# Modulation sums moved from TensorE to VectorE, ScalarE and GpSimd, with longer pauses in background work

## Chip, cores and metric

The kernel runs on one core of one Trainium2 chip. The metric is the device time of one execution in microseconds (us); the figure quoted for a kernel is the median of its runs.

## What is computed

A trunk of two layers works on 256 latent tokens and 256 context tokens of width 1024. Each layer is a gated feed-forward network (FFN), a token-mixing block with four branches (latent attention, windowed attention, a state-space branch called S5, a gated MLP), and a second FFN. Each of these three sub-layers is modulated: a vector made from the conditioning input gives a shift, a scale and a gate of 1024 numbers, one set for latent tokens and one for context tokens. The change concerns how these vectors are made.

```python
mod_l = (silu_c  @ w_ada[l] + b_ada[l]).reshape(b, N_MOD, D_MODEL)      # 9 vectors of 1024 per layer
mod_c = (silu_cc @ w_ada[l][:, :n_mod_c * D_MODEL] + ...)               # 9 in layer 0, 5 in layer 1
def modulated_norm(xs, gain, mod, s):
    return rms_norm(xs, gain) * (1.0 + mod_vec(mod, 3 * s + 1)) + mod_vec(mod, 3 * s)
def gated_residual(xs, y, gain, mod, s, weight):
    return xs + weight * mod_vec(mod, 3 * s + 2) * rms_norm(y, gain)
def ffn_sublayer(xs, mod, s, g_pre, g_post, w_in_f, w_out_f):
    a, g = jnp.split(modulated_norm(xs, g_pre, mod, s) @ w_in_f, 2, axis=-1)
    return gated_residual(xs, (jax.nn.silu(a) * g) @ w_out_f, g_post, mod, s, MACARON_WEIGHT)
```

`w_ada[l]` is 1024 x 9216 in fp32, so each vector reads 4 MB of weights for two rows of activations.

## The kernel before, in words

**Matrix products.** Every large product splits its fp32 operands into a high and a low part and adds three TensorE matmuls (`mm3`, L285 to L287). Weights come in raw tiles of 1 MB over the SP queue (`Ring.pump`, L166). `Ring.ahead` lets ScalarE copy the high part (L208) and VectorE, or GpSimd in the mixing block, subtract it for the low part (L211), up to two pieces ahead of the product that uses them; there are two raw slots and three slots of parts.

**The FFN** (`ffn`, L623) walks 44 blocks of 128 hidden columns. A block is 24 matmuls of 512 columns, and after each half of them `tick` adds 2.6 to `K.clock`. Every second block is followed by `evacuate`: ScalarE SiLU (L655), VectorE product (L659), ScalarE copy (L661), VectorE subtraction (L662). Then `natural_out` multiplies by `w_out`.

**Background work** is written as generators. `tick` (L256) steps each task whose wake time on `K.clock` has come; a task's `yield 2.5` asks for 2.5 of that clock. The clock only orders the program: each engine then runs its own instructions in that order and waits on semaphores. `finish` (L266) steps a task to its end at once.

**Modulation** (`Ada`, L307). A sum over 1024 rows is cut into four chunks of 256 rows. A chunk is one 1 MB load on SP (L320) and four matmuls of 512 columns (L341); the stationary operand holds the two activation columns, and the four matmuls lie side by side in the array. ScalarE evacuates the sum (L347). A shift or scale is then turned by four transposes and two VectorE additions (L364 to L366); a gate goes through four selection matmuls (L382), two VectorE operations (L384, L385) and GpSimd DMAs to DRAM (L388), from where `load_gate` (L392) spreads it. The vectors of sub-layer 0, shift and scale, are made before the first FFN; the other 56 chunks run inside three FFNs: 24 in layer 0's first, 28 in layer 0's second, 12 in layer 1's first; 8 of the 24 are shift and scale of sub-layer 1.

**S5 tables** (`s5_prep`, L1065) are built in the background of each layer's first FFN: VectorE and GpSimd complex products (`cmul`, L98), transposes of the GpSimd results `p_xr` and `p_xi` (L292), and GpSimd DMAs to a DRAM table `tab` (L1129, L1143, L1155). Layer 0's preparation also has the discretisation, of which eight steps are taken ahead of the first FFN. In the mixing block `s5_run` (L1173) reads the table back in four groups `r_tq` (L1189), the first two over SP, and feeds TensorE (L1225). `mla`, `gqa` and `s5_glu` are further background tasks of `mix` (L696).

**Where the time lies.** First FFN about 45 to 460 us, mixing 460 to 890, second FFN 890 to 1330, layer 1's first FFN 1330 to 1745, its mixing 1745 to 2040, its last FFN 2040 to the end.

Of the kernel before, what the change touches and what calls it, by code (L numbers as in the profile page):

```python
# [298 lines left out]
def aux_tile(K):  # L299
    return K.ps_aux.tile([P, 512], F32, tag="aux", name="aux")  # L300
# [6 lines left out]
class Ada:  # L307


    def __init__(self, K, places, jobs):  # L310

        self.K, self.places, self.jobs = K, places, jobs
        self.chunks = [(l, c, k) for l, s, kind, _ in jobs
                       for c in ((3 * s, 3 * s + 1) if kind == "norm" else (3 * s + 2,)) for k in range(0, 8, 2)]
        self.loaded = self.n = 0
# [8 lines left out]
    def run(self, every, bank=aux_tile):  # L324
        self.every, self.bank = every, bank
        self.pump()
        yield every[0]
        for l, s, kind, weight in self.jobs:
            yield from (self.norm(l, s) if kind == "norm" else self.gate(l, s, weight))
# [39 lines left out]
    def gate(self, l, s, weight):  # L369

        K, nc, v, q = self.K, self.K.nc, self.K.nc.vector, self.K.nc.gpsimd
        c0 = (3 * s + 2) * D
        ev = yield from self.sums()
        bp = t2k(K, "bp")
        v.memset(bp, 0.0)
        for st in range(2):
            nc.sync.dma_start(bp[st:st + 97:32, 0:256], K.b_ada[l, c0:c0 + D].rearrange("(q c) -> q c", q=4))
            nc.sync.dma_start(bp[st:st + 97:32, 256:512], K.norm_post[l, s].rearrange("(q c) -> q c", q=4))
        yield 8.0
        pt = self.bank(K)  # L380
        for k in range(4):
            nc.tensor.matmul(pt[32 * k:32 * k + 32, 0:256], K.sel[:, k // 2, :], ev[:, 256 * (k % 2):256 * (k % 2) + 256], start=True, stop=True,  # L382
                             tile_position=(0, 32 * k))
        v.tensor_tensor(out=ev[:, :256], in0=pt[:, :256], in1=bp[:, 0:256], op=OP.add)  # L384
        v.scalar_tensor_tensor(out=ev[:, :256], in0=ev[:, :256], scalar=weight, in1=bp[:, 256:512], op0=OP.mult, op1=OP.mult)  # L385
        gd = K.dr.tile([2, 4, 256], F32, tag=f"gd{l}{s}", name=f"gd{l}{s}")
        for st in range(2):
            q.dma_start(gd[st], ev[st:st + 97:32, :256])  # L388
        K.gd[l, s] = gd
# [233 lines left out]
def ffn(K, l, s, f, pn, tiles, nxt, jobs, every=(5.0, 7.6), pools=None, prep=False):  # L623
# [8 lines left out]
    with pools.es as es:  # L632
        hb = None
        big = [gp.tile([P, 2, 1024], F32, tag=t, name="ada" + t) for t in ("G", "y1")]
        ada = add_task(K, Ada(K, big, jobs).run(every), 5.0)
# [53 lines left out]
        load_gate(K, l, s, G)  # L689
# [6 lines left out]
def mix(K, l, pn, last, nxt):  # L696
# [67 lines left out]

    def u_out(t, p):
# [20 lines left out]
    def s5_all():  # L786
        out = yield from s5_run(K, l, sp5, A, K.tab[l], K.r8d[l], not last)
        yield from s5_glu(K, l, sp5, *out, Tq, new_branch)

    s5t = add_task(K, s5_all(), 2.0)  # L790
# [274 lines left out]
def s5_prep(K, l, pool, tab, loads=None):  # L1065
# [55 lines left out]
    for qg in range(4):  # L1121
# [8 lines left out]
        if qg < 2:  # L1130
# [11 lines left out]
            yield 2.5  # L1142
# [30 lines left out]
def s5_run(K, l, pool, A, tab, r8d, need_ctx):  # L1173
# [18 lines left out]
    load_tq(0)  # L1192
    yield 4.0
# [18 lines left out]
    load_tq(1)  # L1212
# [98 lines left out]
def s5_glu(K, l, pool, ygT, wh, wl, bg, Tq, new_branch):  # L1311
# [8 lines left out]
    yield 2.5  # L1320
# [139 lines left out]
def mla(K, l, pool, wkv, wq, gk, rm, wqs, nB, nC, ntq, new_branch):  # L1460
# [42 lines left out]
    yield 5.0  # L1503
# [71 lines left out]
def gqa(K, l, pool, nB, nC, ntq, new_branch):  # L1575
# [11 lines left out]
    for src, n in ((nC[:, 0:2, 256:512], 256), (nB[:, 0:2, 160:288], P)):  # L1587
# [9 lines left out]
        yield 3.0  # L1597
# [37 lines left out]
def trace(K, nc, tc, rec):  # L1635
# [4 lines left out]
    with ExitStack() as es:  # L1640
# [18 lines left out]
        K.sel = C([P, 2, 32], "sel")  # L1659
# [15 lines left out]
        nc.vector.memset(K.sel, 0.0)  # L1675
        id4 = K.ident.rearrange("p (a b r) -> p a b r", a=2, b=2)
        nc.vector.tensor_tensor(out=K.sel[:, :, 0:2], in0=id4[:, 0, :, 0:2], in1=id4[:, 1, :, 0:2], op=OP.add)
# [6 lines left out]
        for l in range(2):  # L1684
# [6 lines left out]
                  [(0, 0, "norm", None)])  # L1691
        for i, _ in enumerate(ada.run((0.0, 0.0), mm_tile)):
# [10 lines left out]
            for _ in range((1, 1, 1, 1, 2, 2, 0, 0, 0)[min(i, 8)]):  # L1703
                pools.ptask.step(0.0)
# [12 lines left out]
        for l in range(2):  # L1717
            last = l == 1
            jobs = [(0, 0, "gate", 0.5), (0, 1, "norm", None), (0, 1, "gate", 1.0)] if l == 0 else []
            jobs.append((l, 2, "norm", None))  # L1720
            if last:
                jobs.append((l, 2, "gate", 0.5))
            pn = ffn(K, l, 0, 0, pn, range(4), lambda: PreNorm(K, l, 1), jobs, (7.6, 7.6) if last else (5.0, 7.6), pools, True)
            pools = None
            pn = mix(K, l, pn, last, lambda: PreNorm(K, l, 2))
            if last:
                ffn(K, l, 2, 1, pn, range(2), None, [])
            else:
                pn = ffn(K, l, 2, 1, pn, range(4), lambda: PreNorm(K, l + 1, 0), [(l, 2, "gate", 0.5)] + [(l + 1, i, *j) for i, w in ((0, 0.5), (1, 1.0)) for j in (("norm", None), ("gate", w))])
# [65 lines left out]
```

## Time and profile before

| | us |
|---|---|
| median of 3 runs (2238.04 to 2239.87) | 2238.07 |
| the profiled execution's own time | 2238.61 |
| its span, first to last instruction | 2236.8 |
| TensorE busy in it | 2124.8 |
| VectorE busy | 1110.7 |
| ScalarE busy | 764.4 |
| GpSimd busy | 399.5 |

The profile shows one execution. Engines are PE (TensorE matmul), PEld (its weight load), DVE (VectorE), ACT (ScalarE), POOL (GpSimd) and SP (which issues DMAs). "L341" is a line of the kernel. [...]

### The profile page before, as it was taken

The numbers are of one execution on the slowest core, as the hardware profiler recorded it, in microseconds if no ns is written. First come the engines' busy times: TensorE is split into PE (matmuls) and PEld (weight loads), VectorE is DVE, ScalarE is ACT, GpSimd is POOL, SyncE is SP. The second block draws the span as 40 slices with busy tenths as digits, with TensorE's granted clock in tenths as the row PEclk, the third lists the DMA queues.
The fourth block names the chain that finished last, engine by engine and source line by source line (L and its number), as shares of the span: only waits on it lengthen the run. The fifth ranks groups of instructions, "written<-read, shape, count | busy, mean of one in ns | idle before, by whom it ended". The sixth has DMA issues, their size and how long they took to land.

```text
span 2236.8 us, 28936 instructions
## 1 busy us (share of the span) xinstructions
PE 2124.8 (95%) x11691; PEld 1716.4 (77%) x11691; DVE 1110.7 (50%) x1965; ACT 764.4 (34%) x1275; POOL 399.5 (18%) x372
## 2 busy tenths in 40 slices
PE   5899999989999999899999989999999889897998
PEld 3677778877767778777777877778888778787997
DVE  6873332357435655533332357733324585656554
ACT  3222222342533333422222332222222345354443
POOL 1660000022222300100000027500000244442000
PEclk9999999999999999999999998999999999998999
DMA  8566542324322223355554335633323454443554
GB/s 295 179 217 208 184 159 85 128 93 175 98 70 71 83 83 114 114 185 189 173 198 151 114 102 171 228 134 113 104 87 105 168 168 123 125 141 120 182 188 151
DMA packets 211039, 323.12 MB, mean 144 GB/s; under 512 B 15737, under 2 KB 152569, under 8 KB 210905
## 3 DMA queue, kind: packets, MB, share of 16 engines
q1 hardware_dynamic: 196864, 287.17, 38.4%
q0 software_dynamic: 9584, 31.56, 4.3%
q10 hardware_dynamic: 4456, 2.53, 0.5%
q8 instruction: 92, 1.51, 0.3%
q14 instruction: 43, 0.34, 0.0%
HBM read 307.57 MB, written 14.71 MB: 144 GB/s over the span
## 4 chain that ended last, share of the span: by engine, by line
PE 48%; DVE 5%; issue 2%; ACT 1%; DMA 1%; POOL 1%; ACTq 0%; SPq 0%; DVEq 0%; POOLq 0%
PE mm L285 15%; PE mm L286 14%; PE mm L287 14%; PE aux L341 2%; PE aux L292 1%; DMA r_tq<-tab 1%; DVE wlo L211 1%; ACT jk L400 0%; DVE hThi L462 0%; PE aux L1438 0%; ACT h L459 0%; DVE hTlo L463 0%; DVE g_tm L1594 0%; PE aux L1563 0%; DVE xs L433 0%
## 5 line engine op out<-in xcount | busy, mean ns | idle before, releaser
L285 PE MATMUL mm<-hThi,whi 128*128 128x512 f32 (+1 forms) x1992 | 719.6, 361 | 8.7 <-DVE hThi L462 8.4
L286 PE MATMUL mm<-hTlo,whi 128*128 128x512 f32 (+1 forms) x1992 | 703.7, 353 | 7.7 <-POOL hTlo L463 7.3
L287 PE MATMUL mm<-hThi,wlo 128*128 128x512 f32 (+1 forms) x1992 | 701.1, 352 | 0.0
L211 DVE TENSOR_TENSOR wlo<-wraw,whi 128x1024 fp32r<-128x1024 f32 (+1 forms) x285 | 363.2, 1279 | 427.3 <-ACT whi L208 425.6
L285 PEld LDWEIGHTS mm<-hThi,whi 128*128 128x128 f32 x1992 | 382.5, 192 | 119.6 <-issue 49.4
L208 ACT ACTIVATE whi<-wraw 128x1024 fp32r<-128x1024 f32 (+1 forms) x348 | 363.9, 1049 | 237.5 <-PE mm L287 174.5
L286 PEld LDWEIGHTS mm<-hTlo,whi 128*128 128x128 f32 x1992 | 382.3, 192 | 58.7 <-POOL hTlo L463 10.3
L287 PEld LDWEIGHTS mm<-hThi,wlo 128*128 128x128 f32 x1992 | 382.0, 192 | 50.4
L211 POOL TENSOR_TENSOR wlo<-wraw,whi 128x1024 fp32r<-128x1024 f32 (+1 forms) x66 | 162.3, 2467 | 861.4 <-ACT whi L208 821.1
L659 DVE TENSOR_TENSOR sa<-sa,mm 128x512 f32<-128x512 f32 (+1 forms) x88 | 54.3, 617 | 160.2 <-PE mm L287 160.2
L655 ACT ACTIVATE sa<-mm 128x512 f32<-128x512 f32 (+1 forms) x88 | 47.8, 544 | 229.6 <-PE mm L287 229.6
L285 PE MATMUL mm<-whi,ha 128*128 128x512 f32 x308 | 120.0, 389 | 0.0
L286 PE MATMUL mm<-wlo,ha 128*128 128x512 f32 x308 | 119.8, 389 | 0.0
L287 PE MATMUL mm<-whi,ha 128*128 128x512 f32 x308 | 119.8, 389 | 0.0
L661 ACT ACTIVATE ha<-sa 128x512 fp32r<-128x512 f32 (+1 forms) x44 | 25.4, 578 | 228.3 <-DVE sa L659 228.3
L661 ACT ACTIVATE hb<-sa 128x512 fp32r<-128x512 f32 (+1 forms) x44 | 25.4, 578 | 178.3 <-DVE sa L659 169.7
L287 PE MATMUL mm<-whi,hTlo 128*128 128x512 f32 (+2 forms) x224 | 80.9, 361 | 4.4 <-POOL hTlo L463 4.3
L285 PE MATMUL mm<-whi,hThi 128*128 128x512 f32 (+2 forms) x224 | 81.9, 366 | 3.4 <-DVE hThi L462 3.4
L286 PE MATMUL mm<-wlo,hThi 128*128 128x512 f32 (+2 forms) x224 | 80.4, 359 | 1.2 <-DVE wlo L211 1.2
L388 POOL DMA_DIRECT2D gd<-ev x12 | 7.0, 583 | 415.6 <-ACT whi L208 253.4
L285 PE MATMUL mm<-whi,hb 128*128 128x512 f32 x188 | 73.1, 389 | 0.0
L286 PE MATMUL mm<-wlo,hb 128*128 128x512 f32 x188 | 73.1, 389 | 0.0
(446 smaller groups left out, 2909.6 us busy)
## 6 DMA issues: line engine op xcount, KB each, us to landing
wraw<-in_w_ffn_in_dram SPq DMA_DIRECT2D x88, 1024.0 KB
wraw<-in_w_in_dram SPq DMA_DIRECT2D x42, 1024.0 KB
wraw<-in_w_ffn_out_dram SPq DMA_DIRECT2D x40, 1024.0 KB
adaG<-in_w_ada_dram SPq DMA_DIRECT2D x32, 1024.0 KB
aday<-in_w_ada_dram SPq DMA_DIRECT2D x32, 1024.0 KB
ha<-in_w_ada_dram SPq DMA_DIRECT2D x8, 1024.0 KB
wraw<-in_w_out_dram SPq DMA_DIRECT2D x7, 1024.0 KB
r_tq<-tab SPq DMA_DIRECT2D x8, 768.0 KB
```

The lines of the kernel that those rows point to most:

```text
L208: K.nc.scalar.activation(h3, r, AF.Copy)
L211: (self.eng or K.lo_eng).tensor_tensor(out=l3, in0=r, in1=h3.bitcast(F32), op=OP.subtract)
L285: mm(out, ahi, bhi, start=first, stop=False)
L286: mm(out, ahi, blo, start=False, stop=False)
L287: mm(out, alo, bhi, start=False, stop=last)
L292: K.nc.tensor.transpose(out, x, K.ident[:n, :n])
L341: nc.tensor.matmul(ps[o:o + 32, :], self.K.sc[:, k + i, :], w[:, i, 512 * b:512 * b + 512], start=k == 0, stop=k == 6, tile_position=(0, o))
L388: q.dma_start(gd[st], ev[st:st + 97:32, :256])
L655: nc.scalar.activation(sa[:, :N], ps[:, :N], AF.Silu)
L659: nc.vector.tensor_tensor(out=g[:, :N], in0=g[:, :N], in1=ps[:, :N], op=OP.mult)
L661: nc.scalar.activation(hh, g[:, :N], AF.Copy)
```

## The change

Six things change together.

1. `AdaSum` makes 14 of the modulation vectors without TensorE. A step takes 128 rows by 512 columns (256 KB, one SP load into one of four places): VectorE multiplies by the latent activation and adds to an accumulator; for vectors that context tokens need too (`ns` = 2), ScalarE scales the same tile in place and GpSimd adds it to a second accumulator. Sixteen steps make one vector; then `total` sums over partitions with `2 * ns` matmuls against ones. Of the 14, ten have `ns` = 2 and four `ns` = 1. Shift and scale of layer 0's sub-layer 1 stay with `Ada` and go first.
2. Steps are paced by `K.clock`: one per 1.75 in layer 0's first FFN (64 steps), per 1.6 in its second (112 steps, the last 16 with `ns` = 1), per 3.2 in layer 1's first (48 steps, all `ns` = 1).
3. `s5_prep`: the pause ahead of the second group's transposes grows from 2.5 to 11; the `p_xt` table transfers are issued on ScalarE, right after the copy that fills them; five of its steps, not eight, are taken ahead of the first FFN.
4. `s5_run` is started at the head of `mix`, so that the first two table groups are read there.
5. Pauses grow in `s5_glu` (2.5 to 5), `mla` (5 to 10) and `gqa` (3 to 7 for the keys).
6. `load_gate` loads only the streams in use.

```diff
+class AdaSum:
+    def pump(self):
+        while self.loaded < min(self.n + len(self.places), len(self.chunks)):
+            l, c, k, b = self.chunks[self.loaded]
+            c0 = D * c + 512 * b
+            self.K.nc.sync.dma_start(self.places[self.loaded % len(self.places)], self.K.w_ada[l, P * k:P * k + P, c0:c0 + 512])
+            self.loaded += 1
+    def run(self, every):
...
+        due = self.K.clock
+        for l, s, kind, weight, ns in self.jobs:
+            for k in range(8):
+                for b in range(2):
...
+                    if k == 0:
+                        nc.vector.tensor_scalar(out=a[0], in0=w, scalar1=f[0], scalar2=None, op0=OP.mult)
+                    else:
+                        nc.vector.scalar_tensor_tensor(out=a[0], in0=w, scalar=f[0], in1=a[0], op0=OP.mult, op1=OP.add)
+                    if ns > 1:
+                        nc.scalar.activation(w if k else a[1], w, AF.Copy, scale=f[1])
+                        if k:
+                            nc.gpsimd.tensor_tensor(out=a[1], in0=a[1], in1=w, op=OP.add)
+                    self.n += 1
+                    self.pump()
...
+                    due += every
+                    if due > self.K.clock:
+                        yield due - self.K.clock
+            yield 2.5
...
+    def total(self, ns):
+        ps = aux_tile(self.K)
+        for st in range(ns):
+            for b in range(2):
+                o = 64 * st + 32 * b
+                self.K.nc.tensor.matmul(ps[o:o + 32, :], self.K.ones[:, 0:32], self.acc[:, st, 512 * b:512 * b + 512], start=True, stop=True,
+                                        tile_position=(0, o))
+        return ps
...
@@ ffn
-        ada = add_task(K, Ada(K, big, jobs).run(every), 5.0)
+        def modulation():
+            if first:
+                yield from Ada(K, big, first).run((5.0, 7.6))
+            yield from AdaSum(K, [big[0][:, j // 2, 512 * (j % 2):512 * (j % 2) + 512] for j in range(4)], big[1], jobs).run(every)
+        ada = add_task(K, modulation(), 5.0)
...
@@ mix
+    s5g = s5_all()
+    next(s5g)
...
-    s5t = add_task(K, s5_all(), 2.0)
+    s5t = add_task(K, s5g, 6.0)
@@ s5_prep
-            yield 2.5
+            yield 2.5 if qg == 0 else 11.0
...
+        nc.scalar.dma_start(tab[:, gs, 0:256], xt.rearrange("p j k m -> p j (k m)"))
         if qg < 3:
             x = x_table(qg + 1)
         yield 2.5
-        dq.dma_start(tab[:, gs, 0:256], xt.rearrange("p j k m -> p j (k m)"))
@@ s5_run
     load_tq(0)
+    load_tq(1)
     yield 4.0
...
-    load_tq(1)
@@ s5_glu
-    yield 2.5
+    yield 5.0
@@ mla
-    yield 5.0
+    yield 10.0
@@ gqa
-        yield 3.0
+        yield 3.0 if n > P else 7.0
@@ trace, ahead of the first FFN
-            for _ in range((1, 1, 1, 1, 2, 2, 0, 0, 0)[min(i, 8)]):
+            if i in (0, 5, 6, 7, 8):
                 pools.ptask.step(0.0)
```

## Rows read from the trace of the kernel before

**Rows 1.** The page, part 1: busy time, share of the span, instructions.
```profile
PE 2124.8 (95%) x11691; PEld 1716.4 (77%) x11691; DVE 1110.7 (50%) x1965; ACT 764.4 (34%) x1275; POOL 399.5 (18%) x372
```
**Rows 2.** Stretches: length, busy PE, PEld, DVE, ACT, POOL; granted clock; DMA share, GB/s.
```profile
1040.00:1080.00 40.00, 40.00 (x190) 29.53 (x189) 13.83 (x18) 11.45 (x15) 0.00 (x0) 1.00 0.54 185
...
1400.00:1440.00 40.00, 40.00 (x244) 30.27 (x241) 36.55 (x40) 11.70 (x17) 22.46 (x27) 1.00 0.57 187
1440.00:1480.00 40.00, 40.00 (x188) 30.44 (x187) 13.02 (x17) 9.87 (x13) 4.81 (x9) 1.00 0.72 254
...
1600.00:1640.00 40.00, 40.00 (x178) 33.14 (x177) 11.34 (x11) 8.96 (x10) 0.00 (x0) 1.00 0.34 112
```
**Rows 3.** Chain that ended last, around one chunk: start, length, engine and line.
```profile
985.67 1.00 PE aux L341 x8
986.67 0.43 PE mm L285
987.10 0.23 PE mm L286
```
**Rows 4.** Lines L341 and L382: ns min/median/max, first and last start us.
```profile
L341 PE MATMUL aux<-adaG,sc x256: 592/592/617, 58.3 to 1482.8; 128*32 128x512 f32 x128
...
L382 PE MATMUL aux<-ev,sel x48: 379/391/403, 120.6 to 1512.2; 128*32 128x256 f32 x48
```
**Rows 5.** Timeline 1404 to 1412: start, length, engine; in brackets the idle time before.
```profile
1404.16 8.03 DVE L211 TENSOR_TENSOR wlo<-wraw,whi 128x1024 fp32r<-128x1024 f32 x1 [0.26 <-ACT whi L208]
...
1404.52 1.07 POOL L102 TENSOR_TENSOR p_cmg<-p_px,p_B 128x512 f32<-128x512 f32 x1
...
1409.83 1.27 POOL L110 TENSOR_TENSOR p_xi<-p_xi,p_cmgu 128x512 f32<-128x512 f32 x1
```
**Rows 6.** Timeline 1361 to 1366: VectorE while GpSimd works too.
```profile
1362.44 1.76 DVE L102 TENSOR_TENSOR p_cmv<-p_pr,p_C 128x512 f32<-128x512 f32 x1
1364.13 1.77 DVE L103 TENSOR_TENSOR p_cmvu<-p_pr,p_C 128x512 f32<-128x512 f32 x1
```
**Rows 7.** Durations by line, ns min/median/max, of shapes the change adds or meets.
```profile
L211 DVE TENSOR_TENSOR wlo<-wraw,whi x285: 1018/1226/8027, 35.3 to 2222.7; 128x1024 fp32r<-128x1024 f32 x140, 128x832 fp32r<-128x832 f32 x3
...
L662 DVE TENSOR_TENSOR hb<-sa,hb x44: 424/692/693, 223.1 to 2172.3; 128x512 fp32r<-128x512 f32 x33, 128x256 fp32r<-128x256 f32 x11
...
L512 DVE SCALAR_TENSOR_TENSOR x<-z,po_rst,x x20: 751/752/754, 445.9 to 2232.4; 128x512 f32<-128x512 f32 x20
...
L433 DVE TENSOR_SCALAR xs<-x,pn_rst x44: 473/481/2626, 15.4 to 2037.8; 128x512 f32<-128x512 f32 x44
...
L463 POOL TENSOR_TENSOR hTlo<-h,hThi x22: 1258/1276/1394, 37.0 to 2043.9; 128x512 fp32r<-128x512 f32 x22
...
L400 ACT ACTIVATE jk<-x x44: 629/632/637, 10.0 to 2034.7; 128x512 f32<-128x512 f32 x44
```
**Rows 8.** DMA issues: queue, count, KB each, median us from issue to landing.
```profile
wkv<-in_mla_w_ukv_dram POOLq DMA_DIRECT2D x2, 256.0 KB, 3.2
```
**Rows 9.** Table building, TensorE: transposes in both layers and the wait before each.
```profile
112.43 1.11 PE L292 MATMUL aux<-ident,p_xr 128*128 128x128 f32 x4 [9.73 <-POOL p_xr L106]
...
1391.52 1.11 PE L292 MATMUL aux<-ident,p_xr 128*128 128x128 f32 x4 [3.65 <-POOL p_xr L106]
```
**Rows 10.** The same, in stretches: length, busy PE, granted clock, DMA share, GB/s.
```profile
115.00:120.00 5.00, 5.00 (x36) 0.76 0.72 217
...
1390.00:1395.00 5.00, 3.37 (x12) 0.56 0.46 172
```
**Rows 11.** The mixing block: issue of the table reads (ns), and TensorE's waits (us).
```profile
L1189 SPq DMA_DIRECT2D r_tq<-tab x8: 339/427/499, 495.3 to 1766.3; - x8
...
PE px L1225 <- DMA r_tq<-tab: 2.9, 1, 2.9
...
PEld aux L292 <- issue: 6.9, 1, 6.9
...
PEld aux L286 <- DVE g_yl L1319: 1.5, 1, 1.5
```

More of the change, by code (lines that the diff above doesn't have):

```diff
@@ L312, in __init__ @@
         self.K, self.places, self.jobs = K, places, jobs
-        self.chunks = [(l, c, k) for l, s, kind, _ in jobs
-                       for c in ((3 * s, 3 * s + 1) if kind == "norm" else (3 * s + 2,)) for k in range(0, 8, 2)]
+        self.chunks = [(l, c, k) for l, s in jobs for c in (3 * s, 3 * s + 1) for k in range(0, 8, 2)]
         self.loaded = self.n = 0
@@ L327, in run @@
         yield every[0]
-        for l, s, kind, weight in self.jobs:
-            yield from (self.norm(l, s) if kind == "norm" else self.gate(l, s, weight))
+        for l, s in self.jobs:
+            yield from self.norm(l, s)
     def sums(self):
@@ L620, in __init__, with ffn @@
             self.ptask = add_task(K, s5_prep(K, l, pp, K.tab[l], self.loads))
-def ffn(K, l, s, f, pn, tiles, nxt, jobs, every=(5.0, 7.6), pools=None, prep=False):
+def ffn(K, l, s, f, pn, tiles, nxt, jobs, every=1.6, pools=None, prep=False, first=()):
     nc = K.nc
@@ L763, in mix, with s5_all @@
     A = sp5.tile([64, 8, 256], F32, tag="r_A", name="r_A")
+    def s5_all():
+        out = yield from s5_run(K, l, sp5, A, K.tab[l], K.r8d[l], not last)
+        yield from s5_glu(K, l, sp5, *out, Tq, new_branch)
+    s5g = s5_all()
+    next(s5g)
     def u_out(t, p):
@@ L784, in mix @@
         pb.part(t, 0)
-    def s5_all():
-        out = yield from s5_run(K, l, sp5, A, K.tab[l], K.r8d[l], not last)
-        yield from s5_glu(K, l, sp5, *out, Tq, new_branch)
-    s5t = add_task(K, s5_all(), 2.0)
+    s5t = add_task(K, s5g, 6.0)
     pb.run(range(4), 1)
@@ L1658, in trace @@
         K.sc = C([P, 8, 32], "sc")
-        K.sel = C([P, 2, 32], "sel")
+        K.ones = C([P, 64], "ones")
         K.npT = C([P, 2, 3, 8], "npT")
@@ L1674, in trace @@
         nc.scalar.activation(K.sc[:, :, 0:2], pt[:, 0:16].rearrange("p (s b) -> p b s", s=2), AF.Silu)
-        nc.vector.memset(K.sel, 0.0)
-        id4 = K.ident.rearrange("p (a b r) -> p a b r", a=2, b=2)
-        nc.vector.tensor_tensor(out=K.sel[:, :, 0:2], in0=id4[:, 0, :, 0:2], in1=id4[:, 1, :, 0:2], op=OP.add)
+        nc.vector.memset(K.ones, 1.0)
         pt = aux_tile(K)
@@ L1718, in trace @@
             last = l == 1
-            jobs = [(0, 0, "gate", 0.5), (0, 1, "norm", None), (0, 1, "gate", 1.0)] if l == 0 else []
-            jobs.append((l, 2, "norm", None))
+            norm = lambda a, b, ns: [(a, b, "shift", None, ns), (a, b, "scale", None, ns)]
             if last:
-                jobs.append((l, 2, "gate", 0.5))
-            pn = ffn(K, l, 0, 0, pn, range(4), lambda: PreNorm(K, l, 1), jobs, (7.6, 7.6) if last else (5.0, 7.6), pools, True)
+                jobs, first, every = [*norm(1, 2, 1), (1, 2, "gate", 0.5, 1)], (), 3.2
+            else:
+                jobs, first, every = [(0, 0, "gate", 0.5, 2), (0, 1, "gate", 1.0, 2), *norm(0, 2, 2)], ((0, 1),), 1.75
+            pn = ffn(K, l, 0, 0, pn, range(4), lambda: PreNorm(K, l, 1), jobs, every, pools, True, first)
             pools = None
@@ L1728, in trace @@
             else:
-                pn = ffn(K, l, 2, 1, pn, range(4), lambda: PreNorm(K, l + 1, 0), [(l, 2, "gate", 0.5)] + [(l + 1, i, *j) for i, w in ((0, 0.5), (1, 1.0)) for j in (("norm", None), ("gate", w))])
+                jobs = [(l, 2, "gate", 0.5, 2)]
+                for i, w in ((0, 0.5), (1, 1.0)):
+                    jobs += [*norm(l + 1, i, 2), (l + 1, i, "gate", w, 2 - i)]
+                pn = ffn(K, l, 2, 1, pn, range(4), lambda: PreNorm(K, l + 1, 0), jobs)
 def trunk(tc, *args):
```

75 lines of the change are left out of this document (55 added, 20 removed).

## The prediction

> **What bounds the kernel now.** I read the busy times first: TensorE works for 2124.8 us of the 2236.8 us span and no other engine for more than half of it [rows 1]. Cut into stretches of 40 us, the FFNs show TensorE at 40.00 of 40 at full clock with VectorE at 11 to 14, ScalarE at 9 to 11 and GpSimd near 0 [rows 2]. So in an FFN an instruction taken off TensorE is time, as long as the others keep up. What one chunk costs is read from the chain that ended last: the chunk starts at 985.67, the second matmul behind it at 987.10, while two neighbours are 0.23 apart [rows 3]; the chunk holds the stream up by 1.43 - 0.23 = 1.20 us. Then I looked at what VectorE and GpSimd do to each other, because the change makes both work in the FFNs. In the timeline a VectorE subtraction of the usual 1.22 us takes 8.03 and ends at 1412.19, 1.09 us after a run of six GpSimd products that began at 1404.52 and ended at 1411.10 [rows 5, 7]: it stood still for the whole run. Where the two alternate, VectorE's 128x512 products, elsewhere near 0.69 us [rows 7], take 1.76 and end 1.70 apart, a GpSimd product and a VectorE product in turn [rows 6]. Operations with two tensors from SBUF on the one engine and on the other exclude each other here. TensorE never stopped in that stretch (40.00 of 40, VectorE "busy" 36.55) [rows 2], so a VectorE lag of 8.03 - 1.22 = 6.8 us is absorbed by the weight parts made two pieces ahead.
>
> My sum is made against the profiled execution, 2238.6 us (span 2236.8 and 1.8 around it), 0.5 us above the median.
>
> **TensorE's work.** 56 chunks leave: 56 x 1.20 = -67.2. Each of the 14 vectors gets one sum over partitions, at most four fp32 matmuls of 512 columns side by side like a chunk [rows 4], 1.20 each: +16.8. (Four have half of that; I leave them at the full price.) The six gates lose four selection matmuls of 256 columns, 8 of the 48 instructions [rows 4], each set priced at 0.84, between 0.39 (one instruction) and 1.20 (a chunk): -5.0. The transposes stay in number. Together **-55.4**.
>
> **What the new steps cost elsewhere.** With `ns` = 2 a vector has 16 steps; 14 of them are a VectorE multiply-add of two SBUF tensors (nearest row 0.75) and a GpSimd add (1.28); in two VectorE only multiplies (0.48) and GpSimd does nothing [rows 7]. ScalarE's 0.63 per step [rows 7] shares nothing. By the alternating rows a pair takes less than its parts: 1.70 where 0.69 + 1.28 is 1.97, so 0.27 less; I price the pair at 0.75 + 1.28 - 0.27 = 1.76. The mean step is (14 x 1.76 + 2 x 0.48) / 16 = 1.60 us of VectorE and GpSimd together. A block of the FFN is 24 matmuls, and 178 matmuls take 40 us [rows 2]: 5.39 us for 5.2 on the program's clock, 1.037 us each. A block needs besides a weight subtraction (1.22) and half a hidden subtraction (0.35) [rows 7]: 1.57.
> - Layer 0's first FFN: 5.2 / 1.75 = 2.97 steps, 2.97 x 1.60 + 1.57 = 6.32 against 5.39. The 64 steps last 112 of clock, 21.5 blocks: 21.5 x 0.93 = 20.0 too much.
> - Its second: 3.25 steps, 6.77 against 5.39, over 96 steps = 29.5 blocks: 40.7 too much. The last 16 steps have no GpSimd part.
> - Layer 1's first: no GpSimd at all, 1.6 steps x 0.75 + 1.57 = 2.8 of 5.39: hidden.
>
> Of each excess 6.8 us is absorbed, as read above: 13.2 + 33.9 = 47.1. Within a block the engines also wait for each other in order (VectorE for ScalarE's copy, ScalarE's scaling for VectorE, the load for GpSimd), which costs only where both stand idle; I take **+50**, next to the sum of the rows. The bounds: 0, if the lag never uses up the lookahead, and +95, if the ring of four places sets the pace (second rival).
>
> What queues behind these waits: behind the multiply-add on VectorE the weight and hidden subtractions; behind the scaling on ScalarE SiLU and the weight copies; behind the add on GpSimd the gate's DMAs and, early on, table building; on SP each 256 KB load waits for the add that frees its place, and the weight loads stand behind it. The DMA rate is no bound: 256 KB x 3.25 per 5.39 us is 158 GB/s, and weights at 1 MB per two blocks 97; 254 GB/s is what one stretch already moved, at a share of 0.72 [rows 2]. SP issues four times as many loads, 224 for 56, each near 0.43 us [rows 11], about a quarter of its time.
>
> **Table building.** TensorE waits 9.73 us for GpSimd's `p_xr` in layer 0 and 3.65 in layer 1 [rows 9]. Behind each the granted clock is at the lower of its two levels: 0.76 over 115 to 120 [rows 10] is half speed for 2.4 us, and with the 2.6 us from the transposes to 115 some 5.0 us at half, 2.5 lost; in layer 1 half speed for about 3.5 us, 1.7 lost. The pause is 8.5 longer, 8.8 us of other matmuls: layer 0 keeps 0.9 of its wait, -11; layer 1 none, -5. Together **-16**; bounds 0 (the wait returns one group later) and -18. The eight `p_xt` issues leave GpSimd's queue and cost ScalarE about 0.43 us each [rows 11], beside other work.
>
> **Mixing.** The table reads are issued some 20 us earlier, when SP has no weight load due; layer 1's wait of 2.9 goes [rows 11], layer 0's I put at 2 (0 to 2.9). If SP were held by buffers not yet free, weight loads behind it would be late; 0 is the bound. The wait of 6.9 before the key transposes [rows 11] shrinks by 4 x 1.037: -4. `s5_glu`'s 1.5 [rows 11] goes only if the task is not already being finished at once, when pauses count for nothing: -1 (0 to -1.5). `mla`'s longer pause may leave attention work to be stepped without cover in layer 1: +1 (0 to +4). Together **-9**.
>
> **Start.** Three preparation steps move into the first FFN, where VectorE stands ahead of the context normalisation. No row prices them; between -2 and +5, by the 3.45 of 40 us that VectorE had left in its fullest stretch [rows 2], I take **+2**.
>
> Sum: -55.4 + 50 - 16 - 9 + 2 = -28.4, so 2238.6 - 28.4 = **2210 us**, 1.3% faster. About 0.2%, 4.5 us, is what a measurement of this kernel can tell from no change.
>
> **Rivals.**
> - *The excess does not bite.* Then the sum is -78.4: 2160. For it: VectorE lags of 6.8 us that cost TensorE nothing [rows 2, 5]. Against it: the excess comes in every block, not once. 0.18.
> - *Slower: the ring of four places.* The place of step n is loaded again only when its add is done, and VectorE waits at the head of its queue for the load. A round is load 3.2 [rows 8], 0.75, 0.63 and 1.28 [rows 7], and two waits for the other engine (1.28 and 1.22): 8.4 us for four steps, 2.1 each; a load behind a 1 MB weight load (some 4 us at 254 GB/s) makes a round 12.4. At 2.4 us a step 160 steps take 384 against 160 x 1.721 (1.75 and 1.6 weighted, x 1.037) = 275; less 13.6 absorbed, +95: 2255. It turns slower than before at (275 + 13.6 + 78.4) / 160 = 2.30 us a step. For it: the 2.1 is close. Against it: the load overlaps the other three places. 0.20.
> - *The pauses only move the waits.* Without 16 of table building and the 5 of `gqa` and `s5_glu`: 2231. For it: GpSimd's backlog in both layers; against it: nothing late follows within the added pause. 0.09.
> - *Multiply-adds at half rate.* The row has 0.75 for two fp32 SBUF tensors, against 0.69 for a plain subtraction [rows 7]. At twice the 0.69 an `ns` = 2 step would take 0.6 more: 140 x 0.63 = 88, and 2298. The trace speaks against it: 0.03. [...]
>
> **How the numbers follow.** 0.50 for the forecast; its own range, with port waits of 35 to 65 and the bounds above, is 2190 to 2230. The range 2162 to 2250 leaves out the ends of the first two rivals and the last one. Faster: nearly all of the forecast (0.48), the first rival (0.18), half of the third (0.05): 0.71. Slower: 0.21, the second and fourth rivals but for 0.02. Same: 0.08.
>
> **What would show it.** L341 falls from 576 matmul instructions to 128. In layer 0's two FFNs TensorE has gaps before matmuls that wait for VectorE's weight part, about 14 and 35 us in all, and many VectorE rows of 1.8 to 2.0 us; in layer 1's first FFN none. GpSimd's add rows are near 1.28, or stretched. The `p_xr` waits shrink to under 1 us. If the gaps are absent, or a multiply-add waits for its load more than for GpSimd, my cost of the steps is wrong; so too if `p_xr` waits come back in a later group.

## The result, and the profile after

The changed kernel takes **2272.5 us** (median of 4 runs, 2271.5 to 2273.5) where the kernel before took 2238.1 in the same session: a ratio of 1.0154, 95% interval 1.0137 to 1.0172. It is 1.5% slower. The forecast was 2210, the range ended at 2250.

The profiled span is 2270.6 us, 33.8 more than before. The page of the changed kernel, part 1 (busy time, share of the span, instructions), against [rows 1]:

```profile
PE 2112.3 (93%) x11291; PEld 1713.2 (75%) x11291; DVE 1329.0 (59%) x2174; ACT 866.0 (38%) x1429; POOL 611.1 (27%) x513
```

TensorE has 400 instructions fewer, yet its busy time fell by only 12.5 us, and its idle time (the span less the busy time) grew from 112.0 to 158.3. Where it waits is told by the waits of TensorE (engine, tile, line, what it waited for; us in all, times, longest):

```profile
PE aux L425 <- DVE aday L401: 32.5, 14, 4.7
...
PE mm L285 <- ACT whi L208: 14.4, 3, 8.5
...
PE aux L425 <- POOL aday L405: 11.2, 14, 1.3
...
PE aux L292 <- POOL p_xr L106: 8.5, 1, 8.5
...
PE aux L425 <- issue: 4.1, 1, 4.1
...
PE mm L287 <- DVE wlo L211: 2.1, 4, 0.8
```

L425 is the sum over partitions. Its waits make 47.8 us; the weight parts on VectorE (`wlo`), where the prediction had put the loss, make 2.1. The groups of instructions (busy us, mean ns of one; idle time of the engine before them) say the same, and that the means of the new operations are longer than the rows that they were priced from (0.75 for the multiply-add, 1.28 for the add):

```profile
L211 DVE TENSOR_TENSOR wlo<-wraw,whi 128x1024 fp32r<-128x1024 f32 (+1 forms) x285 | 392.8, 1383 | 366.7 <-ACT whi L208 365.4
...
L405 POOL TENSOR_TENSOR aday<-aday,adaG 128x512 f32<-128x512 f32 x140 | 213.7, 1552 | 143.5 <-ACT adaG L403 143.5
...
L401 DVE SCALAR_TENSOR_TENSOR aday<-adaG,sc,aday 128x512 f32<-128x512 f32 x196 | 170.9, 913 | 23.5 <-DMA adaG<-in_w_ada_dram 23.5
...
L425 PE MATMUL aux<-aday,ones 128*32 128x512 f32 x96 | 51.4, 752 | 47.9 <-DVE aday L401 32.5 <-POOL aday L405 11.2 <-issue 4.1
```

In these rows `wlo` is the low weight part on VectorE (L211) and `aday` (L401, L405) are the accumulators of the new sums. The median multiply-add takes 743 ns, as an undisturbed one (746 in e5 below); the mean of 913 comes from those that are held up, the longest 7.9 us.

One stall at the table building of layer 0, and one in layer 0's second FFN, in the timeline (start, length, engine, line; in brackets the idle time before and who ended it):

```profile
95.31 0.39 PE L287 MATMUL mm<-hThi,wlo 128*128 128x512 f32 x1
95.88 4.84 POOL L104 TENSOR_TENSOR p_xr<-p_px,p_B 128x512 f32<-128x512 f32 x1
...
104.17 1.11 PE L292 MATMUL aux<-ident,p_xr 128*128 128x128 f32 x4 [8.47 <-POOL p_xr L106]
...
985.04 0.39 PE L287 MATMUL mm<-hThi,wlo 128*128 128x512 f32 x1
...
985.91 4.46 POOL L405 TENSOR_TENSOR aday<-aday,adaG 128x512 f32<-128x512 f32 x3 [1.45 <-ACT adaG L403]
...
986.39 1.05 PE L425 MATMUL aux<-aday,ones 128*32 128x512 f32 x2 [0.96 <-DVE aday L401]
...
987.64 1.60 DVE L751 TENSOR_TENSOR ha<-sa,ha 128x512 fp32r<-128x512 f32 x1 [0.71 <-ACT ha L750]
989.17 2.28 DVE L211 TENSOR_TENSOR wlo<-wraw,whi 128x1024 fp32r<-128x1024 f32 x1
991.37 0.74 DVE L401 SCALAR_TENSOR_TENSOR aday<-adaG,sc,aday 128x512 f32<-128x512 f32 x1
...
992.16 1.92 PE L425 MATMUL aux<-aday,ones 128*32 128x512 f32 x4 [4.73 <-DVE aday L401]
...
994.33 1.53 PE L425 MATMUL aux<-aday,ones 128*32 128x512 f32 x2 [0.24 <-POOL aday L405]
...
995.78 0.50 PE L285 MATMUL mm<-hThi,whi 128*128 128x512 f32 x1
```

From the last weight matmul at 985.04 to the next at 995.78 TensorE does nothing but one vector's sum: 10.7 us for what was priced at 1.20. The last multiply-add (991.37) stood in VectorE's queue behind a subtraction of the hidden tile of 1.60 us and a weight part of 2.28 (0.69 and 1.23 undisturbed [rows 7]). Three adds of GpSimd run from 985.91 to 990.37; the weight part begins at 989.17 and ends at 991.45, 1.08 us after the last of them. Behind the sum in TensorE's queue stands the whole FFN. The matmuls come as 2, 4 and 2 instructions, as their accumulators get ready, and no longer side by side. The clock suffers too; stretches of the same place (length, busy PE, PEld, DVE, ACT, POOL, granted clock, DMA share, GB/s):

```profile
977.00:989.00 12.00, 9.47 (x40) 6.78 (x38) 9.07 (x9) 6.99 (x10) 9.09 (x7) 0.98 0.66 201
989.00:1001.00 12.00, 8.60 (x29) 4.71 (x30) 9.42 (x12) 3.83 (x6) 4.72 (x6) 0.74 0.58 176
1001.00:1013.00 12.00, 12.00 (x55) 9.94 (x54) 6.42 (x8) 7.45 (x11) 8.85 (x7) 1.00 0.65 202
```

VectorE is busy for 9.4 of 12, its standing still included (the weight part of 2.28 us for 1.23 counts whole), so it isn't full: it is late. The granted clock is 0.74 over the 12 us: by single microseconds 0.50 from 989 to 995 and 1.00 from 996 on. The traces of both kernels have no levels but these two.

The theory from here: the sums expose every lag of VectorE and GpSimd, and the lag comes from the two excluding each other. Rivals: the other parts of the change; the hand-over of a place from VectorE to ScalarE to GpSimd; the ring of four places into which the steps' tiles are loaded.

### The profile page after: what moved, and what is told of

It is laid out like the page before. It is cut to its first block, busy times and chain, and to the rows that moved or that the text cites. A ratio compares the mean times of both kernels' runs of the same rounds, so it can differ in the third digit from the quotient of the medians.

```text
span 2270.6 us, 29371 instructions
## 1 busy us (share of the span) xinstructions
PE 2112.3 (93%) x11291; PEld 1713.2 (75%) x11291; DVE 1329.0 (59%) x2174; ACT 866.0 (38%) x1429; POOL 611.1 (27%) x513
## 5 line engine op out<-in xcount | busy, mean ns | idle before, releaser
L211 DVE TENSOR_TENSOR wlo<-wraw,whi 128x1024 fp32r<-128x1024 f32 (+1 forms) x285 | 392.8, 1383 | 366.7 <-ACT whi L208 365.4
L211 POOL TENSOR_TENSOR wlo<-wraw,whi 128x1024 fp32r<-128x1024 f32 (+1 forms) x66 | 161.4, 2454 | 837.4 <-ACT whi L208 788.7
L405 POOL TENSOR_TENSOR aday<-aday,adaG 128x512 f32<-128x512 f32 x140 | 213.7, 1552 | 143.5 <-ACT adaG L403 143.5
L401 DVE SCALAR_TENSOR_TENSOR aday<-adaG,sc,aday 128x512 f32<-128x512 f32 x196 | 170.9, 913 | 23.5 <-DMA adaG<-in_w_ada_dram 23.5
L403 ACT ACTIVATE adaG<-adaG,sc 128x512 f32<-128x512 f32 x140 | 96.9, 724 | 169.7 <-DVE aday L401 169.6
L425 PE MATMUL aux<-aday,ones 128*32 128x512 f32 x96 | 51.4, 752 | 47.9 <-DVE aday L401 32.5
```

The costliest lines, as they stand in the source:

```text
L211: (self.eng or K.lo_eng).tensor_tensor(out=l3, in0=r, in1=h3.bitcast(F32), op=OP.subtract)
L401: nc.vector.scalar_tensor_tensor(out=a[0], in0=w, scalar=f[0], in1=a[0], op0=OP.mult, op1=OP.add)
L403: nc.scalar.activation(w if k else a[1], w, AF.Copy, scale=f[1])
L405: nc.gpsimd.tensor_tensor(out=a[1], in0=a[1], in1=w, op=OP.add)
L425: self.K.nc.tensor.matmul(ps[o:o + 32, :], self.K.ones[:, 0:32], self.acc[:, st, 512 * b:512 * b + 512], start=True, stop=True, tile_posit ...
```

## The experiments

All ratios are to the kernel before on the same chip; it had 2239.7 to 2240.4 us there, and 2238.1 beside the changed kernel. So a difference between two runs of different sessions, as most below are, is good to some 2 us, and by the intervals of the ratios to some 5.

**Which part costs.** `e1_sums_alone` is the changed kernel with every other edit undone, `e2_rest_alone` the kernel before with every edit but the sums.

> The changed kernel with only its modulation sums kept: pauses, table transfers, early table reads and the steps ahead of the first FFN are as before. Theory (the sums over partitions stand in TensorE's order too close behind accumulators that come late): nearly all of the loss is in this part, so 2265 to 2285 us, slower than the changed kernel by the 12 us that the mixing changes gave; TensorE's idle time in front of the sums near 48 us in all. Rival (the loss comes from the other parts: the later preparation steps, the transfers on ScalarE's queue, the pauses): 2205 to 2225 us, faster than before.

> The kernel before with everything of the change but the modulation sums: the chunks stay on TensorE. Theory: faster than before by what mixing gave (12 us), less some 5 us at the start; 2222 to 2234 us. The wait for p_xr that moved one group earlier shows here too, if the later preparation steps made it. Rival (the other parts are at fault): 2255 to 2270 us.

Measured: e1 2279.9 us (1.0182 [1.0166, 1.0198]), e2 2227.0 us (0.9945 [0.9929, 0.9962]). Both as the theory said: the sums cost 39.5 us, the rest gains 13.4. In e2 the 8.5 us wait for `p_xr` is there without any of the new sums.

**The distance of a sum from its last step.**

```diff
-            yield 2.5
+            yield 8.0
             if kind == "gate":
```

> The changed kernel with 8.0 of clock between a vector's last step and its sum over partitions, for 2.5. The mean pace of the steps is as it was, since each step has a due time and the late ones are stepped in a row. Theory (the sum only stands too close): the idle time in front of the sums falls from 48 us to under 12, and the time to 2225 to 2240 us. Rival (VectorE and GpSimd have more to do than an FFN has time for, whatever the distance): the steps that are stepped in a row behind each pause carry the lag over to the next sum and to the weight parts; 2262 to 2285 us.

Measured: 2258.8 us (1.0087 [1.0072, 1.0102]), between the two expectations, 13.6 better than the changed kernel. TensorE's waits, and the sum's group:

```profile
PE mm L285 <- ACT whi L208: 49.3, 14, 8.5
...
PE mm L287 <- DVE wlo L211: 14.3, 17, 3.0
```

```profile
L425 PE MATMUL aux<-aday,ones 128*32 128x512 f32 x96 | 15.5, 605 | 0.0
```

The sums wait for nothing and take 15.5 us for 14, 1.1 each, near the 1.20 of the prediction. But `whi` has 34.9 us more than in the changed kernel and `wlo` 12.2 more: 47.1, as much as the sums had waited. The wait moved to the weight parts nearly whole: TensorE is idle for 155.1 us of the span, for 158.3 in the changed kernel. The gain is in its work: the sums' matmuls take 35.9 us less, of which 10.0 are left in the total busy time (2102.3 us for 2112.3), at a mean granted clock of 0.966 for 0.972. Placement explains 13.6 us; the lag is real.

**Taking the second stream's steps away.**

```diff
-                    if ns > 1:
-                        nc.scalar.activation(w if k else a[1], w, AF.Copy, scale=f[1])
-                        if k:
-                            nc.gpsimd.tensor_tensor(out=a[1], in0=a[1], in1=w, op=OP.add)
+                    if ns > 1 and k == 0:
+                        nc.scalar.activation(a[1], w, AF.Copy, scale=f[1])
```

> The changed kernel without the context stream's scalings on ScalarE and adds on GpSimd after its first product (the context's modulation vectors are left out in this way; the sums over partitions stay, with four matmuls each). Theory: without GpSimd's adds VectorE is not held, the accumulators are done in time, the idle time in front of the sums falls from 48 us to under 8, and with the clock that they cost the time is 2205 to 2222 us. Rival (a sum costs TensorE its 10 us because of what it is, four matmuls that don't run side by side, and not because of what it waits for): 2245 to 2265 us.

Measured: 2187.5 us (0.9771 [0.9754, 0.9788]), 85 less than the changed kernel and below the band of the theory. Of the waits in front of sums 7.4 us are left. So the scalings and adds of the context stream, which run on no engine that is full, cost 85 us. (This run, and e8 and e13 to e15 below, leave the context's sums out: they show a cost, and are no kernel to use.)

**Both streams on VectorE**, with neither ScalarE nor GpSimd:

```diff
-                        nc.scalar.activation(w if k else a[1], w, AF.Copy, scale=f[1])
-                        if k:
-                            nc.gpsimd.tensor_tensor(out=a[1], in0=a[1], in1=w, op=OP.add)
+                        if k == 0:
+                            nc.scalar.activation(a[1], w, AF.Copy, scale=f[1])
+                        else:
+                            nc.vector.scalar_tensor_tensor(out=a[1], in0=w, scalar=f[1], in1=a[1], op0=OP.mult, op1=OP.add)
```

> The changed kernel with the context stream's steps as a second multiply-add on VectorE, without ScalarE and GpSimd. Theory of the lock (VectorE and GpSimd exclude each other, 1.76 us a pair): a step is 1.5 us of VectorE alone and nothing else holds VectorE, but a block of layer 0's second FFN still asks 3.25 x 1.5 + 1.57 = 6.4 us of it in 5.39, so two thirds of the loss stay: 2240 to 2260 us, VectorE's weight rows back near 1.22 us. Rival (the loss comes from the hand-over, VectorE to ScalarE to GpSimd on one place, since ScalarE scales the place where VectorE must have read it): with one engine there is no hand-over, and the time falls to 2195 to 2220 us.

Measured: 2239.4 us (0.9993 [0.9983, 1.0003]), 0.6 under the lock theory's band and 19 above the rival's. One engine doing all of it is 33 us better than three sharing it. Over 975 to 1200 us, groups of instructions of this run:

```profile
L401 DVE SCALAR_TENSOR_TENSOR aday<-adaG,sc,aday 128x512 f32<-128x512 f32 x84 | 61.9, 746 | 9.7 <-DMA adaG<-in_w_ada_dram 9.7
...
L211 DVE TENSOR_TENSOR wlo<-wraw,whi 128x1024 fp32r<-128x1024 f32 x34 | 41.6, 1223 | 21.7 <-ACT whi L208 21.7
```

These are undisturbed durations; in the changed kernel the same stretch has 938 and 1516 ns.

**The hand-over.** ScalarE scales a place in place, so it must wait until VectorE has read it (170 us of ScalarE's waits). `e9_no_hand_over` gives it a tile of its own:

```diff
-                        nc.scalar.activation(w if k else a[1], w, AF.Copy, scale=f[1])
+                        z = t2k(self.K, "az") if k else a[1]
+                        nc.scalar.activation(z, w, AF.Copy, scale=f[1])
                         if k:
-                            nc.gpsimd.tensor_tensor(out=a[1], in0=a[1], in1=w, op=OP.add)
+                            nc.gpsimd.tensor_tensor(out=a[1], in0=a[1], in1=z, op=OP.add)
```

> The changed kernel with ScalarE scaling into a tile of its own, not into the place, so that it needs not wait until VectorE has read the place; GpSimd adds that tile. Theory of the lock: VectorE and GpSimd have as much to do as before and exclude each other as before, 2255 to 2285 us. Rival (hand-over): ScalarE's waits for the multiply-add (170 us in all) go, its weight copies are no longer behind them, and the time falls to 2215 to 2245 us.

Measured: 2277.2 us (1.0163 [1.0148, 1.0178]): no gain. Over 975 to 1200 us:

```profile
L406 POOL TENSOR_TENSOR aday<-aday,az 128x512 f32<-128x512 f32 x78 | 128.6, 1673 | 64.3 <-ACT az L404 64.1
L401 DVE SCALAR_TENSOR_TENSOR aday<-adaG,sc,aday 128x512 f32<-128x512 f32 x85 | 126.1, 1532 | 5.9 <-DMA adaG<-in_w_ada_dram 5.9
```

Of ScalarE's waits for the multiply-add 5.5 us are left in this stretch, for 88.9 in the changed kernel, and the multiply-add has become 1532 ns instead (938 there). My reading, which no run isolates, is that the two engines, freed from each other's order, meet more often and take turns. VectorE waits 5.9 us for loads here, so it is not the ring that holds it; ScalarE, which now runs ahead, waits 45.2 us for them.

**What in GpSimd's step excludes VectorE.** Three runs replace the add: by a copy (`e8_one_source`), by two copies (`e13_two_copies`), by three memsets of the place (`e15_three_memsets`); `e14_two_copies_own_tile` is two copies in the form of e9.

```diff
-                            nc.gpsimd.tensor_tensor(out=a[1], in0=a[1], in1=w, op=OP.add)
+                            nc.gpsimd.tensor_copy(a[1], w)
```

```diff
-                            nc.gpsimd.tensor_tensor(out=a[1], in0=a[1], in1=w, op=OP.add)
+                            nc.gpsimd.memset(w, 0.0)
+                            nc.gpsimd.memset(w, 0.0)
+                            nc.gpsimd.memset(w, 0.0)
```

> The changed kernel with GpSimd copying the scaled place to the accumulator where it added it (the context's modulation vectors are left out in this way): the same hand-over, order and queue, but GpSimd reads one tensor where it read two. Theory of the lock: two-tensor operations exclude each other, a copy does not; VectorE's multiply-adds return to 0.75 us and its weight rows to about 1.28, the idle time in front of the sums falls from 48 us to under 12, and the time to 2190 to 2215 us. Rival (the hand-over costs it): the waits stay, 2250 to 2275 us.

> The changed kernel with two GpSimd copies of 0.69 us in place of each add (the context's modulation vectors are left out in this way): GpSimd is busy per step as long as with an add (1.38 for 1.28 us unhindered), but reads one tensor at a time. Theory of the lock: VectorE's multiply-adds stay near 0.8 us and its weight rows near 1.32, the time is 2214 to 2232 us. Rival (GpSimd's time per step, not the exclusion, made the accumulators late): the waits in front of the sums come back, 2250 to 2275 us.

> As the run with two GpSimd copies per step (the context's modulation vectors are left out), but ScalarE scales into a tile of its own and GpSimd copies from that, so that a place comes free for its next load without GpSimd. Theory A (a copy of GpSimd and a two-tensor operation of VectorE hold each other up too, if less than two two-tensor ones): the loss stays, 2250 to 2275 us, and VectorE's multiply-adds stretch. Theory B (the chain of load, VectorE, ScalarE and GpSimd on one place was what made two copies as slow as an add): without it 2215 to 2235 us.

> The changed kernel with three GpSimd memsets of the place (each near 0.5 us, together 1.56 us a step, as long as an add took) instead of each add (the context's modulation vectors are left out): GpSimd reads nothing, but the place comes free for its load as late as before. Theory A (GpSimd's reading beside VectorE's is the trouble): VectorE's rows are as undisturbed as with both streams on VectorE (multiply-add 0.75, weights 1.22 us in layer 0's second FFN) and the time is 2195 to 2225 us. Theory B (the place comes free late, so the ring of four sets the pace): 2245 to 2275 us, with VectorE's multiply-adds waiting for loads over 60 us.

Measured: e8 2216.2 us (0.9890 [0.9876, 0.9905]), in time just over the lock theory's band, with 775 ns for the multiply-adds, 1225 for the weight parts and 14.6 us of waits in front of sums; e13 2259.6 us (1.0090 [1.0072, 1.0108]), in its rival's band; e14 2233.9 us (0.9966 [0.9954, 0.9979]), in theory B's band; e15 2225.6 us (0.9935 [0.9920, 0.9950]), just over theory A's band and far from theory B's. The theory as I had stated it, two-tensor operations on both sides, fell with e13. The timeline of e13 shows why:

```profile
980.36 0.61 POOL L406 COPY aday<-adaG 128x512 f32<-128x512 f32 x1
...
981.52 1.54 DVE L211 TENSOR_TENSOR wlo<-wraw,whi 128x1024 fp32r<-128x1024 f32 x1
982.05 1.49 POOL L406 COPY aday<-adaG 128x512 f32<-128x512 f32 x1
982.99 1.09 DVE L401 SCALAR_TENSOR_TENSOR aday<-adaG,sc,aday 128x512 f32<-128x512 f32 x1
```

A copy reads one tensor and takes 0.61 us where nothing stands before it; behind VectorE's weight part, which ends at 983.06, it takes 1.49, and the multiply-add that overlaps its end takes 1.09 for 0.75. A copy takes part in the exclusion. Over 975 to 1200 us of e14:

```profile
L401 DVE SCALAR_TENSOR_TENSOR aday<-adaG,sc,aday 128x512 f32<-128x512 f32 x84 | 79.8, 994 | 11.0 <-DMA adaG<-in_w_ada_dram 10.8
L406 POOL COPY aday<-az 128x512 f32<-128x512 f32 x70 | 67.0, 957 | 27.1 <-ACT az L404 27.1
```

and of e15:

```profile
L401 DVE SCALAR_TENSOR_TENSOR aday<-adaG,sc,aday 128x512 f32<-128x512 f32 x84 | 60.1, 748 | 24.3 <-DMA adaG<-in_w_ada_dram 24.1
...
L211 DVE TENSOR_TENSOR wlo<-wraw,whi 128x1024 fp32r<-128x1024 f32 x36 | 44.1, 1226 | 43.1 <-ACT whi L208 43.1
...
L405 POOL MEMSET adaG<- 128x512 f32 x70 | 36.6, 522 | 38.1 <-ACT adaG L403 38.0
```

Three memsets keep GpSimd as busy as an add (1.57 us a step for 1.55) and the place as long, but VectorE's rows are undisturbed and the kernel is 47 us faster than the changed one. So of the 85 us up to 47 go with GpSimd's reading. Not all need be its doing: the memsets write the place and not the accumulator, so that the sums of e15 need not wait for GpSimd either, for which those of the changed kernel waited 11.2 us. What the runs show is that copies, which read, and VectorE's two-tensor operations hold each other up (a copy of 0.61 us takes 1.49 in e13), and that memsets, which only write, leave VectorE as it was (beside those of e15 the multiply-add takes 748 ns, and 746 in e5, which has no step of GpSimd).

The other 38 (2225.6 - 2187.5) come with what is left of the step: ScalarE's scaling, GpSimd's time, during which the place is held, and the order in which the three engines wait for each other; sums still wait 25.5 us in e15. GpSimd's time counts by itself: e8, which reads but has one copy of 0.69 us a step, is 43 us faster than e13 with two and 9 faster than e15 without reading. Which of these waits they hang on isn't settled. Giving ScalarE its own tile gained 26 us with copies (e13 to e14), although the multiply-adds grew from 869 to 994 ns, and nothing with adds; so the order and the exclusion are not independent, and a stretched multiply-add is not by itself lost time.

**The other parts.** `e7_mixing_and_pause` is the kernel before with the mixing edits and the pause of 11.0, without the moved preparation steps and ScalarE's transfers.

> The kernel before with the mixing changes and the longer pause in table building alone: chunks on TensorE, preparation steps and the issues of the table transfers as before. Theory (in the run of everything but the sums, the later preparation steps cost about 5 us at the start and put the 8.5 us wait for p_xr one group earlier): without them the start is as before and the longer pause takes the waits of 9.7 and 3.7; 2208 to 2220 us. Rival (the wait for p_xr comes whatever the start, since GpSimd is behind): 2222 to 2230 us.

Measured: 2220.5 us (0.9908 [0.9894, 0.9923]), half a microsecond over the theory's band and 6.5 better than e2 (8 by the ratios). The waits for GpSimd's `p_xr` are gone, as the theory said; but between 60 and 140 us TensorE now has this one:

```profile
PE mm L285 <- ACT whi L208: 6.2, 1, 6.2
```

**A version meant to be better**, from both streams on VectorE. `e11_vectore_pause_5` puts 5.0 of clock in front of the sums and undoes the start and the transfers. `e10_shared` besides leaves the shift and scale vectors of later FFNs to TensorE in layer 0, paces the steps otherwise (2.25 and 2.1 of clock in layer 0) and begins layer 1's 75 of clock later (part of the edit):

```diff
-            yield 2.5
+            yield 5.0
...
-                    due += every
+                    due += every * ns / 2
...
-                jobs, first, every = [*norm(1, 2, 1), (1, 2, "gate", 0.5, 1)], (), 3.2
+                jobs, first, every, rest = [*norm(1, 2, 1), (1, 2, "gate", 0.5, 1)], (), 4.8, 75.0
...
-                jobs, first, every = [(0, 0, "gate", 0.5, 2), (0, 1, "gate", 1.0, 2), *norm(0, 2, 2)], ((0, 1),), 1.75
+                jobs, first, every, rest = [(0, 0, "gate", 0.5, 2), (0, 1, "gate", 1.0, 2)], ((0, 1), (0, 2)), 2.25, 0.0
```

> Both streams on VectorE for all 14 vectors, 5.0 of clock in front of a sum, preparation and table transfers as before the change. Theory (VectorE's load, 6.4 us of a 5.39 us block in layer 0's second FFN, is what is left of the loss without the lock): the waits in front of the sums go, but half of them come back behind the weight parts; with some 6 us from the start 2212 to 2228 us. Rival (only the place of the sums was wrong): all 31 us of waits go and the start's 6: 2196 to 2208 us.

> A version meant to beat both: the mixing changes and the longer pause in table building are kept, preparation and table transfers are as before; in layer 0 the four shift and scale vectors of later FFNs stay chunks on TensorE (a chunk every 5 of clock) and only the gates are summed by multiply-adds, both streams on VectorE, at 2.25 and 2.1 of clock a step and half that for one stream; layer 1's three vectors begin 75 of clock later, behind table building; 5.0 of clock in front of each sum. Theory: VectorE is asked for less than a block's 5.39 us and nothing locks it, so TensorE's saving comes whole: 8 vectors leave, 32 chunks x 1.20 = -38, 8 sums +10, six gates' selections -5, from the 2220.5 of the mixing changes and pause alone: 2180 to 2197 us. Rival (closer chunk loads make weight loads late, or the sums still wait): 2205 to 2225 us.

Measured: e11 2219.1 us (0.9909 [0.9893, 0.9924]); e10 **2190.6 us** (0.9783 [0.9766, 0.9800]). Both in the theory's bands. e10 beats both kernels, 2.2% under the one before. Its page, part 1, its waits in front of the sums, and two stretches of layer 0's second FFN:

```profile
PE 2092.2 (95%) x11435; PEld 1706.9 (78%) x11435; DVE 1228.4 (56%) x2140; ACT 765.8 (35%) x1277; POOL 407.1 (19%) x381
```

```profile
PE aux L426 <- DVE aday L401: 3.3, 2, 2.6
```

```profile
953.00:1033.00 80.00, 80.00 (x385) 57.15 (x384) 23.78 (x29) 19.72 (x26) 0.00 (x0) 1.00 0.62 205
1033.00:1113.00 80.00, 80.00 (x362) 64.39 (x361) 54.72 (x76) 25.04 (x34) 3.29 (x6) 1.00 0.53 174
```

TensorE is busy all of these 160 us at full clock, with GpSimd almost silent. e10 changes several things at once; only the later start in layer 1 can be told apart, from e11.

## Why the prediction was wrong, point by point

The profiled executions can be cut into the parts of the program at VectorE's last multiply-add of a residual (`x<-y,po_rst,x`) in each; it starts at 474.36, 920.50, 1331.38, 1744.07 and 2033.74 us in the kernel before, at 498.63, 940.44, 1374.55, 1784.88 and 2066.84 in the changed one. Lengths in us:

| | before | e2, rest alone | changed | e4 | e11 | e10 |
|---|---|---|---|---|---|---|
| start and layer 0's first FFN | 474.4 | 477.4 | 498.6 | 459.2 | 467.2 | 461.8 |
| layer 0's second FFN | 410.9 | 411.2 | 434.1 | 387.5 | 414.2 | 403.6 |
| layer 1's first FFN | 412.7 | 410.5 | 410.3 | 410.8 | 410.3 | 398.2 |
| mixing, both layers | 735.8 | 723.3 | 723.8 | 723.6 | 720.4 | 725.2 |

- **TensorE's work, -55.4: borne out.** A sum out of the way of late accumulators takes 1.1 us (e3) for the 1.20 priced, and e10 gained 30 us over e7 where the same prices give 33.
- **The excess, +50: the step that failed**, in place and in size. By the prices of the prediction the 55.4 are 16.1, 27.7 and 11.6 in the three FFNs of the table; against e2 the changed kernel has +21.2, +22.9 and -0.2. So the new steps cost 37, 51 and 11 us, together 99 for the 50. The prediction said that of each FFN's excess "6.8 us is absorbed" by weight parts made two pieces ahead, and put the rest, 14 and 35 us, in front of weight matmuls. A sum has no such lookahead, only the 2.5 of clock in the program: its last multiply-add stands behind all that VectorE has in its queue, and the sum holds TensorE's whole queue. So in layer 0's FFNs 16.3 and 27.4 us of idle time stand in front of L425, and 2.1 in all in front of `wlo`. That these two come near the 14 and 35 is partly luck, since they wait for something else. What the prediction left out is what a late sum does besides: the sums were priced as work alone, 16.8 us for the 14, and their matmuls took 51.4, as they came one after another and partly at the lower clock (26 of the 96 at a granted clock of 0.50, 1.06 us each; 58 at 1.00, 0.59 to 0.62). With the 47.8 of waits that is 82 of the 99; the rest I have not taken apart. The range calls this +50 "port waits": no run shows a port, only rows that stretch beside GpSimd's (1.22 us to 8.03 [rows 5, 7], 0.75 to a mean of 913 ns here).
- **Two prices in that step.** The block price of 1.57 counted the hidden subtraction but not the product before it, `sa` (line 748 of the changed kernel), 675 ns by its median and half a one per block: 0.34 x 51 blocks = 17 us that the same sum would have added. And the pair was priced as if VectorE and GpSimd took turns smoothly, while of the 85 us that the second stream costs (e4) 38 are left when GpSimd reads nothing (e15). ScalarE, priced as sharing nothing, does not stretch: its 140 scalings in place take 721 to 728 ns, though not the 0.63 of the row.
- **Layer 1's first FFN, "hidden": wrong.** None of its 11.6 us came. Its steps have no GpSimd part of their own, but they begin during table building, where GpSimd's products run. In the changed kernel, as in [rows 5], VectorE stands still for them:

```profile
1447.09 9.07 DVE L401 SCALAR_TENSOR_TENSOR aday<-adaG,sc,aday 128x512 f32<-128x512 f32 x2
...
1449.01 1.07 POOL L102 TENSOR_TENSOR p_cmg<-p_px,p_B 128x512 f32<-128x512 f32 x1
...
1454.33 1.28 POOL L110 TENSOR_TENSOR p_xi<-p_xi,p_cmgu 128x512 f32<-128x512 f32 x1
```

  TensorE waits 8.5 us behind ScalarE's weight copy and 4.1 in front of a sum there. e10, which begins these steps behind table building, has 398.2 us, 12.3 under e7's 410.5; e11, with the same pause and preparation but the early start (and a slower pace, 3.2 of clock a step for 2.4), has 410.3. A `whi` wait of 6.2 us at table building is left in e10.
- **Table building, -16, and start, +2: together near nothing.** In e2 the first row of the table is 3.0 longer and layer 1's first FFN 2.2 shorter than before. The rival that the pauses only move the waits was right in layer 0: the later preparation steps put the wait into group 0, which has no longer pause (8.47 us at 95.7 to 104.2; [rows 9] had 9.73 a group later). e2 shows it, e7 not. Without them the pause's wait goes, but 6.2 us come back behind `whi`. The three moved steps and ScalarE's transfers cost 6.5 us (e2 less e7); which of the two, no run tells. A reading was off too: in layer 1 the work behind the wait is slow from 1391.5 to 1397.5 in the trace of before (matmuls of 0.63 us for 0.39, granted clock 0.50 up to 1397), about 6 us at the lower clock where the prediction had 3.5.
- **Mixing, -9: right, a little small.** The two blocks take 12.0 us less (12.5 in e2). The waits for `r_tq` (2.2 and 2.9 us) are gone, as is the 6.9 before the key transposes.
- **The ring of four** had the sign, not the mechanism. Multiply-adds waited 23.5 us for loads in all; with memsets they waited 43.5 and the kernel was 47 us faster; in e9 they waited 7.7 and it was no faster. That a place is held long does cost something: freeing it earlier gave 26 us with copies (e13 to e14).
- **Half rate** fell: 0.74 us at 991.37 for a multiply-add of two fp32 tensors, 744 to 748 ns on average wherever nothing disturbs it (e4, e5, e10, e15). Twice the 0.69 of the plain subtraction, as that rival had it, does not show for this form here.

By measured parts: the sums +39.5 alone (e1) and the rest -13.4 (e2) make +26 of the +34; the 8 left, not much more than the intervals allow, would be those parts' effect on each other, which I have not taken apart.

## What to carry to other kernels

An instruction that waits for background work must be as far from it in its engine's queue as that work can be late, or the wait stops the bound engine (47.8 us in front of the sums here); but a longer distance alone moved the wait (47.1 us more in front of the weight parts in e3), while without the lag it went (7.4 us left in e4). Before handing work to a second engine, ask which operations of the first it will exclude: here one engine alone with 1.5 us a step was 33 us better than three engines sharing it. Give the helpers only as many steps as fit into a block of the bound engine with all that they already do in it, begin them when no other engine's work holds them up, and leave the rest where it was: of the kernels here that do all the work, that version was the fastest.

## What the runs showed of the hardware that I had not expected

- A GpSimd copy (one SBUF tensor read) and a VectorE operation on two SBUF tensors hold each other up: 0.61 us becomes 1.49, 0.75 becomes 1.09 (e13). GpSimd memsets left VectorE's rows as they were (748 and 1226 ns in e15, 746 and 1223 in e5).
- With the order between the engines loosened (e9), multiply-adds of 938 ns became 1532 and the time stayed.
- Four fp32 matmuls of 512 columns that are side by side when their operands are ready (14 sums in 15.5 us in e3) take 51.4 in the changed kernel, where the operands come one after another, beyond 47.8 us of idle time. Part of this is the lower clock: the mean matmul takes 752 ns there for 605, 1.06 us at a granted clock of 0.50.
